# A two-layer encoder on one core: three moves in the order of the feed-forward blocks

## The chip, the core and the metric

The kernel runs on one core of one Trainium2 chip. A core has a matrix engine (PE), which multiplies and writes into PSUM banks (the kernel uses eight), a vector engine (DVE), an engine for activations and copies (ACT), a general engine (POOL), and SyncE (SP), which issues transfers. Each takes its instructions in program order and waits on semaphores of the others. The metric is the device time of one launch in microseconds (us), lower is better. Before the change the median of three runs is 2026.74 us (2025.84 to 2027.5).

## What is computed

Two layers act on 512 tokens of 1024 features. Each is a feed-forward block, a mixer, a memory attention and a second feed-forward block. The change touches only the feed-forward blocks, of which there are four:

```python
def swiglu(x, wg, wu, wd):
    return (jax.nn.silu(x @ wg) * (x @ wu)) @ wd

h = x
for layer in range(DEPTH):
    g, wg, wu, wd = ffn1[layer]
    h = h + 0.5 * swiglu(rmsnorm(h, g), wg, wu, wd)
    ...                       # mixer and memory attention
    g, wg, wu, wd = ffn2[layer]
    h = h + 0.5 * swiglu(rmsnorm(h, g), wg, wu, wd)
```

The inner width is 2816, that is 22 blocks of 128 units.

## The kernel before, in words

All activations are kept transposed, with features on the partitions and 512 tokens along a row. Every factor of a product is split into a high part and a low remainder (`wh`, `wl`, `xh`, `xl`, `t1h`, `t1l` and so on). A product is three products: high by high, low by high, high by low. The high part is an ACT copy, the low part a DVE subtraction that needs it.

A feed-forward block (`ffn`, with the prefixes l0_ffn1, l0_ffn2, l1_ffn1 and l1_ffn2 in the order of the program) walks over the 22 inner blocks in 11 pairs. Pair 0 is the plain pair: `plain_pair` multiplies it directly and leaves four PSUM banks (a gate and an up bank for each of two blocks), and `plain_end` scales the gate banks by the token factor `R` into `gs`, after which `hidden` applies silu and multiplies by the up banks. Pairs 1 to 10 save one of eight products by sums of quarters, of weights and of tokens. Each of their seven products is 24 matmuls of 128x256 (six groups of four). For a pair they are:

- `open_pair`: product "11" into bank y; ACT then copies that bank away, because y goes on collecting;
- `sum_pair`: product "1" into bank z (weights s, the sum of two quarters, made by a DMA that adds), and product "2" into y (the same s less a quarter, "second sum");
- `cross_pair`: product "21" into a bank x, product "3" into y;
- `close_pair`: product "4" into y (`lower`), product "22" into z (`upper`), then the gate of the pair.

In the trace product "1" has t1h and t1l as its first factor, "2" has t2h, "3" has t3h, "4" has t4h, and "11", "21" and "22" have xh and xl. In pair 1 the copy of y after product "11" goes straight into a quarter of the pair's result tile `gu` (L592). That tile has two buffers of one tag with `tq`, where the sums of tokens are made, so the copy also waits until `t1l` and `t2l` (L486, L488) have been made from it. In later pairs the copy goes into a PSUM bank (L595).

Between the pairs stand down products: `hh` and `hl`, the two parts of the hidden values, times the down weights `wd`, block by block into a bank (L844). The last chunk of eight inner blocks belongs to pairs 7 to 10. Its first output block has own tiles for its weights (`sh`, `sl`); in the last round `ffn` multiplies it by pairs 7 and 8, then by pair 9, the last but one, whose `hh` and `hl` have just been made (L453, L457), and then calls `close_pair` for pair 10, the final one.

What sets the order: on PE it is the order of the code. The other engines are ordered by a scheduler at build time, in which blocks under `high_priority` go ahead and `behind(ins)` keeps an instruction after another one. Three of the four blocks (all but l1_ffn1) come after an attention stage; the code calls these chained, and there the token sums of the new block are late and stand on DVE and ACT among the work of the first pair.

## Time and profile before

| What | us |
|---|---|
| median of three runs | 2026.74 (2025.84 to 2027.5) |
| the profiled execution, its own time | 2023.98 |
| span of the profiled execution, first to last instruction | 2022.0 |
| PE busy in it | 2004.7 |
| DVE busy | 1598.9 |
| ACT busy | 1278.4 |
| POOL busy | 350.0 |
| PE waiting for another engine, all groups listed | 12.0 |

The profiled execution's time is its span and 1.98 us around it, and it is 2.76 us under the median of the runs. PE is busy for 99% of the span and carries the chain of work that ended last almost alone. So a time is changed by what PE waits for, or by how fast its clock lets it go, and the profile is read there: the list of PE's waits first, then a timeline of the places where they fall.

A line of the timeline gives the start in us from the span's start, the duration, the engine, the line of code, the operation with its output and inputs, the shape and the count, and in brackets how long the engine had been idle before it and who released it. Some rows hold several instructions in a row.

### The profile page before, as it was taken

The numbers are of one execution on the slowest core, as the hardware profiler recorded it, in microseconds if no ns is written. First come the engines' busy times: TensorE is split into PE (matmuls) and PEld (weight loads), VectorE is DVE, ScalarE is ACT, GpSimd is POOL, SyncE is SP. The second block draws the span as 40 slices with busy tenths as digits, with TensorE's granted clock in tenths as the row PEclk, the third lists the DMA queues.
The fourth block names the chain that finished last, engine by engine and source line by source line (L and its number), as shares of the span: only waits on it lengthen the run. The fifth ranks groups of instructions, "written<-read, shape, count | busy, mean of one in ns | idle before, by whom it ended". The sixth has DMA issues, their size and how long they took to land.

```text
span 2022.0 us, 35264 instructions
## 1 busy us (share of the span) xinstructions
PE 2004.7 (99%) x13853; PEld 1840.3 (91%) x13853; DVE 1598.9 (79%) x2370; ACT 1278.4 (63%) x1955; POOL 350.0 (17%) x332
## 2 busy tenths in 40 slices
PE   9999999999999999999999999999999999999999
PEld 7999998888888889999989999988888888999997
DVE  8979776699676798888689798774668688979884
ACT  7766564557785566665557665645768566667572
POOL 1011001355521111000010101003453011010100
PEclk9999999999999999999999999999999999999999
DMA  7787755222331187776557877644224325777762
GB/s 234 195 218 191 197 166 160 91 89 84 103 122 64 62 237 186 207 199 170 155 176 208 209 195 198 178 139 138 84 79 136 94 74 153 205 205 197 193 183 91
DMA packets 102262, 316.52 MB, mean 157 GB/s; under 512 B 11472, under 2 KB 14672, under 8 KB 102096
## 3 DMA queue, kind: packets, MB, share of 16 engines
q1 hardware_dynamic: 85680, 257.12, 39.2%
q0 software_dynamic: 16128, 56.63, 16.2%
q8 instruction: 109, 1.79, 0.4%
q10 hardware_dynamic: 288, 0.52, 0.1%
q14 instruction: 57, 0.47, 0.1%
HBM read 301.64 MB, written 12.58 MB: 155 GB/s over the span
## 4 chain that ended last, share of the span: by engine, by line
PE 94%; DVE 3%; ACT 1%; issue 1%; DMA 0%; POOL 0%; SPq 0%; ACTq 0%; DVEq 0%; POOLq 0%
PE ps_pa L569 35%; PE ps_pb L569 14%; PE ps_pa L967 13%; PE ps_pa L913 5%; PE ps_pb L844 4%; PE ps_pa L844 4%; PE ps_pa L401 3%; PE ps_pb L1080 3%; PE ps_pa L1570 2%; PE ps_pa L1401 2%; PE ps_pb L913 2%; PE ps_pb L1133 2%; PE ps_pb L1106 1%; PE ps_pa L1300 1%; PE ps_pb L401 1%; DVE wl L546 1%
## 5 line engine op out<-in xcount | busy, mean ns | idle before, releaser
L169 ACT ACTIVATE wh<-wf 128x1024 fp32r<-128x1024 f32 (+1 forms) x155 | 154.5, 1003 | 175.8 <-issue 37.8
L544 ACT ACTIVATE wh<-s 128x1024 fp32r<-128x1024 f32 (+1 forms) x132 | 136.4, 1035 | 135.3 <-DVE s L611 43.9
L546 DVE TENSOR_TENSOR wl<-s,wh 128x1024 fp32r<-128x1024 f32 (+1 forms) x132 | 157.1, 1190 | 37.0 <-ACT wh L544 36.0
L544 ACT ACTIVATE wh<-wf 128x1024 fp32r<-128x1024 f32 (+1 forms) x132 | 134.7, 1020 | 75.5 <-PE ps_pa L569 48.0
L546 DVE TENSOR_TENSOR wl<-wf,wh 128x1024 fp32r<-128x1024 f32 (+1 forms) x132 | 154.4, 1172 | 27.2 <-ACT wh L544 27.2
L171 DVE TENSOR_TENSOR wl<-wf,wh 128x1024 fp32r<-128x1024 f32 (+1 forms) x110 | 128.7, 1175 | 41.9 <-ACT wh L169 40.1
L544 ACT ACTIVATE sh<-s 128x1024 fp32r<-128x1024 f32 (+1 forms) x92 | 94.1, 1023 | 66.9 <-PE ps_pa L569 24.6
L171 POOL TENSOR_TENSOR wl<-wf,wh 128x1024 fp32r<-128x1024 f32 (+1 forms) x45 | 99.9, 2221 | 204.9 <-ACT wh L169 142.9
L638 POOL DMA_DIRECT2D s<-l_ffn_wq x40 | 35.2, 879 | 542.9 <-ACT s L637 363.0
L546 DVE TENSOR_TENSOR sl<-s,sh 128x1024 fp32r<-128x1024 f32 (+1 forms) x92 | 108.1, 1176 | 22.7 <-ACT sh L544 22.4
L967 PE MATMUL ps_pa<-wh,xh 128*128 128x512 f32 x384 | 121.7, 398 | 0.0
L967 PE MATMUL ps_pa<-wh,xl 128*128 128x512 f32 x384 | 118.9, 391 | 0.0
L967 PE MATMUL ps_pa<-wl,xh 128*128 128x512 f32 x384 | 118.7, 390 | 0.0
L569 PE MATMUL ps_pa<-xh,wh 128*128 128x256 f32 x560 | 86.9, 276 | 0.0
L569 PE MATMUL ps_pa<-xl,wh 128*128 128x256 f32 x560 | 86.9, 276 | 0.0
L569 PE MATMUL ps_pa<-xh,wl 128*128 128x256 f32 x560 | 86.9, 276 | 0.0
L967 PEld LDWEIGHTS ps_pa<-wh,xl 128*128 128x128 f32 x384 | 72.1, 188 | 15.7
L967 PEld LDWEIGHTS ps_pa<-wl,xh 128*128 128x128 f32 x384 | 72.0, 188 | 15.5
L1095 ACT ACTIVATE e<-e,m 128x128 f32<-128x128 f32 (+3 forms) x128 | 70.7, 554 | 21.7 <-DVE m L1094 21.3
L967 PEld LDWEIGHTS ps_pa<-wh,xh 128*128 128x128 f32 x384 | 69.2, 188 | 12.3
L569 PEld LDWEIGHTS ps_pa<-xl,wh 128*128 128x128 f32 x560 | 74.2, 188 | 0.0
L569 PEld LDWEIGHTS ps_pa<-xh,wl 128*128 128x128 f32 x560 | 74.2, 188 | 0.0
(454 smaller groups left out, 6054.1 us busy)
## 6 DMA issues: line engine op xcount, KB each, us to landing
wf<-l_ffn_wq SPq DMA_DIRECT2D x120, 512.0 KB, 4.2
s<-l_ffn_wq SPq DMA_DIRECT2D x80, 512.0 KB, 4.6
s<-l_ffn_wq POOLq DMA_DIRECT2D x80, 512.0 KB, 7.4
wf<-l_w_in SPq DMA_DIRECT2D x48, 512.0 KB, 3.4
wf<-l_ffn_wd SPq DMA_DIRECT2D x32, 512.0 KB, 3.7
wf<-l_ffn_wdq SPq DMA_DIRECT2D x24, 512.0 KB, 4.3
wf<-l_ffn_wdq SPq DMA_DIRECT2D x24, 384.0 KB, 3.6
s<-l_ffn_wdq SPq DMA_DIRECT2D x16, 512.0 KB, 4.5
```

The lines of the kernel that those rows point to most:

```text
L169: self.leading = nc.scalar.activation(wh[:, sl], w[:, sl], AF.Copy)
L171: eng.tensor_sub(wl[:, sl], w[:, sl], wh.bitcast(F32)[:, sl])
L401: nc.tensor.matmul(p, w[a][:, k * P:(k + 1) * P], xs[k][c], start=k == order[0] and a == c == 0, stop=k == order[-1] and a == 1)
L544: self.leading = nc.scalar.activation(h, t, AF.Copy)
L546: self.parted = nc.vector.tensor_sub(l, t, h.bitcast(F32))
L569: self.nc.tensor.matmul(bank[:, z * 256:z * 256 + 256], w[a][:, o:o + P], xs[k][b], start=first and n == 0, stop=n == len(ops) - 1, skip_g ...
L844: self.nc.tensor.matmul(bank, w[a][:, j * P:(j + 1) * P], h, start=j == a == e == 0 and c < len(CHUNKS) - 1, stop=j == nb - 1 and (a, e) = ...
L913: nc.tensor.matmul(banks[dd], w[g, k // 2][a][:, o:o + P], parts(k)[b], start=k == first and a == b == 0, stop=k == last and a == 1)
L967: nc.tensor.matmul(banks[j], xs[k][a][:, j * P:(j + 1) * P], w[b][:, kk * 512:kk * 512 + 512], start=k == a == b == 0, stop=k == KB - 1 an ...
L1080: nc.tensor.matmul(bank[:, o:o + n], a, b[:, :n], start=c == 0, stop=c == len(ops) - 1)
L1095: nc.scalar.activation(e, e, AF.Exp, bias=m[:, i:i + 1], scale=-1.0, accum_out=rs[:, i:i + 1])
L1133: nc.tensor.matmul(p[:, q0:q0 + n], vp[jb][:, h * P:(h + 1) * P], t[:, src:src + n], start=c == 0, stop=c == 7)
```

## The change

Three edits in the feed-forward blocks.

First, the copy of pair 1's y bank goes to a tile `sq` (the tag of the squares, two buffers) in place of the corner of `gu`, under high priority; the later addition of product "21" reads it there. For the other pairs the copy keeps its place in PSUM and gets the same priority.

Second, the plain pair's gate (`gs` from banks and `R`, then silu and the products) is no longer queued by `plain_end`, which only makes `R` and leaves a function `f.gate`. `ffn` calls it after `sum_pair`, behind `f.lowered`, the low part of pair 1's second sum. `f.low(...)` of pair 2 is called a few lines later.

Third, in the last round, `close_pair` of the final pair stands ahead of the down products of pair 9.

```diff
@@ ffn
-                    self.down_products(c, early, LEAD + REST, False, range(CHUNKS[c] - 4, CHUNKS[c] - 2))
                     self.close_pair(pair, True)
+                    self.down_products(c, early, LEAD + REST, False, range(CHUNKS[c] - 4, CHUNKS[c] - 2))
                     self.down(c, early)
@@ plain_end
-        for b in range(2):
-            f.gated = nc.vector.tensor_mul(gs[:, b * S:(b + 1) * S], banks[b][0], f.R)
-        self.hidden(0, gs, [pp[1] for pp in banks])
+        def gate(after):
+            with self.behind(after):
+                for b in range(2):
+                    f.gated = nc.vector.tensor_mul(gs[:, b * S:(b + 1) * S], banks[b][0], f.R)
+            self.hidden(0, gs, [pp[1] for pp in banks])
+        f.gate = gate
@@ open_pair
-        if p == 1:
-            nc.scalar.copy(self.corner(pair, 0, 0), self.halves(pair.y))
-        else:
-            pair.x = self.bank("pa")
-            nc.scalar.copy(pair.x, pair.y)
+        with self.tc.high_priority():
+            if p == 1:
+                pair.x = self.xp.tile([P, S], F32, name="sq", tag="sq", bufs=2)
+                nc.scalar.copy(pair.x, pair.y)
+            else:
+                pair.x = self.bank("pa")
+                nc.scalar.copy(pair.x, pair.y)
@@ sum_pair
-            if p == 2:
-                f.low(f.lowered)
             f.lowered = self.parted
+            if p == 2:
+                f.low(f.lowered)
@@ cross_pair
-            nc.vector.tensor_add(c, c, self.halves(x))
+            nc.vector.tensor_add(c, self.halves(pair.x), self.halves(x))
```

The first place is DVE in pair 1 of l0_ffn1, from the low part of the token sum "2" on. `s1` holds the sums of pair 1 (its second `wl` is the low part of the second sum), `wf` a quarter as loaded, `s3` the sum for product "3", and `gs` the plain pair's gate. Before:

```order
L486 TENSOR_TENSOR t2l_440<-tq_318,t2h_438 128x1024
L424 TENSOR_TENSOR gs_383<-ps_pa_193,R_377 128x512
L424 TENSOR_TENSOR gs_383<-ps_pa_255,R_377 128x512
L486 TENSOR_TENSOR t3l_513<-tq_319,t3h_511 128x1024
L546 TENSOR_TENSOR wl_443<-s1_402,wh_442 128x1024
L546 TENSOR_TENSOR sl_474<-wf_471,sh_473 128x1024
L546 TENSOR_TENSOR wl_508<-s3_503,wh_507 128x1024
L486 TENSOR_TENSOR t4l_583<-tq_319,t4h_581 128x1024
L434 TENSOR_TENSOR gs_383<-t_386,ps_pa_194 128x512
L434 TENSOR_TENSOR gs_383<-t_386,ps_pb_256 128x512
L661 TENSOR_TENSOR s1_402<-wf_471,s1_402 128x1024
L546 TENSOR_TENSOR wl_545<-wf_542,wh_544 128x1024
```

The same twelve instructions after the change:

```order
L491 TENSOR_TENSOR t2l_424<-tq_318,t2h_422 128x1024
L551 TENSOR_TENSOR wl_427<-s1_386,wh_426 128x1024
L551 TENSOR_TENSOR sl_475<-wf_472,sh_474 128x1024
L427 TENSOR_TENSOR gs_384<-ps_pa_193,R_378 128x512
L427 TENSOR_TENSOR gs_384<-ps_pa_255,R_378 128x512
L491 TENSOR_TENSOR t3l_514<-tq_319,t3h_512 128x1024
L551 TENSOR_TENSOR wl_509<-s3_504,wh_508 128x1024
L491 TENSOR_TENSOR t4l_584<-tq_319,t4h_582 128x1024
L668 TENSOR_TENSOR s1_386<-wf_472,s1_386 128x1024
L551 TENSOR_TENSOR wl_546<-wf_543,wh_545 128x1024
L439 TENSOR_TENSOR gs_384<-t_457,ps_pa_194 128x512
L439 TENSOR_TENSOR gs_384<-t_457,ps_pb_256 128x512
```

The low part of the second sum and that of the quarter for "21" have moved ahead of the gate's first two products and of t3l, and the gate's last two products have moved behind the low part for the next pair's "11".

The second place is ACT over the same stretch, where `ps_pa_340` is bank y of pair 1 and `t` the silu of the plain pair. Before:

```order
L483 ACTIVATE t4h_581<-tq_319 128x1024
L544 ACTIVATE sh_473<-wf_471 128x1024
L544 ACTIVATE wh_442<-s1_402 128x1024
L544 ACTIVATE wh_507<-s3_503 128x1024
L592 COPY gu_374<-ps_pa_340 128x2x256
L432 ACT_TABLE_LOAD
L432 ACTIVATE t_386<-gs_383 128x1024
L544 ACTIVATE wh_544<-wf_542 128x1024
L619 COPY gu_374<-ps_pa_340 128x2x256
```

And after:

```order
L488 ACTIVATE t4h_582<-tq_319 128x1024
L549 ACTIVATE sh_474<-wf_472 128x1024
L599 COPY sq_375<-ps_pa_340 128x512
L549 ACTIVATE wh_426<-s1_386 128x1024
L549 ACTIVATE wh_508<-s3_504 128x1024
L549 ACTIVATE wh_545<-wf_543 128x1024
L626 COPY gu_374<-ps_pa_340 128x2x256
L437 ACT_TABLE_LOAD
L437 ACTIVATE t_457<-gs_384 128x1024
```

The copy of y has moved ahead of the high parts of the second and third sums, and the table load with the silu behind the next pair's first high part and the second copy of y.

The third place is PE in the last round. `ps_pa<-hh,sh` are down products, `ps_pb<-xh,wh` begins product "22" of the final pair, and `t4h` is in its product "4". Before:

```order
L844 MATMUL ps_pa<-hh,sl 128x512 x4
L844 MATMUL ps_pa<-hh,sh 128x512 x2
L844 MATMUL ps_pa<-hl,sh 128x512 x2
L844 MATMUL ps_pa<-hh,sl 128x512 x2
L569 MATMUL ps_pb<-xh,wh 128x256 x4
```

And after, at the end of that pair:

```order
L574 MATMUL ps_pa<-t4l,wh 128x256 x4
L574 MATMUL ps_pa<-t4h,wl 128x256 x4
L851 MATMUL ps_pa<-hh,sh 128x512 x2
L851 MATMUL ps_pa<-hl,sh 128x512 x2
L851 MATMUL ps_pa<-hh,sl 128x512 x2
```

The six down products of pair 9 have moved behind the 48 matmuls that close the final pair. This is the only move on PE; it is made in all four blocks.

## The prediction

> **What bounds the kernel now.** I read the page first: busy time, then the chain that ended last.

> ```profile
> PE 2004.7 (99%) x13853; PEld 1840.3 (91%) x13853; DVE 1598.9 (79%) x2370; ACT 1278.4 (63%) x1955; POOL 350.0 (17%) x332
> PE 94%; DVE 3%; ACT 1%; issue 1%; DMA 0%; POOL 0%; SPq 0%; ACTq 0%; DVEq 0%; POOLq 0%
> ```

> PE is the bound, and the change removes no matmul. What it can win is time in which PE waits, so the next view is the list of waits, PE alone (total us, times, longest):

> ```profile
> PE ps_pa L569 <- ACT gu L592: 5.0, 3, 1.7
> PE ps_pa L569 <- DVE wl L546: 2.7, 3, 0.9
> PE ps_pa L844 <- DVE hl L457: 1.8, 4, 0.5
> PE ps_pa L569 <- ACT gu L644: 0.5, 1, 0.5
> ```

> These make 10.0 us, and all of them lie where the change works. The first two fall together, once in each chained block; the timeline of l0_ffn1 shows how:

> ```profile
> 32.94 1.04 ACT L544 ACTIVATE sh<-wf 128x1024 fp32r<-128x1024 f32 x1
> 35.49 1.22 DVE L486 TENSOR_TENSOR t2l<-tq,t2h 128x1024 fp32r<-128x1024 f32 x1
> 35.60 2.01 ACT L544 ACTIVATE wh<-s 128x1024 fp32r<-128x1024 f32 x2 [1.63 <-DVE s L611]
> 36.63 1.28 DVE L424 TENSOR_TENSOR gs<-ps_pa,R 128x512 f32<-128x512 f32 x2
> 37.52 0.56 ACT L592 COPY gu<-ps_pa 128x512 f32<-128x512 f32 x1
> 38.13 0.73 PE L569 MATMUL ps_pa<-t2h,wh 128*128 128x256 f32 x4 [1.66 <-ACT gu L592]
> 38.96 1.22 DVE L546 TENSOR_TENSOR wl<-s,wh 128x1024 fp32r<-128x1024 f32 x1
> 40.23 0.72 PE L569 MATMUL ps_pa<-t2h,wl 128*128 128x256 f32 x4 [0.91 <-DVE wl L546]
> ```

> PE had finished product "1" at 38.13 - 1.66 = 36.47. Product "2" adds to bank y, so it waited for ACT to copy y away, and that copy stood behind two high parts. Then it waited for the low part of its weights, which on DVE stood behind the gate's first two products and t3l.

> A stall has a second price in the third chained block, l1_ffn2. The chain has the same 112 matmuls after the stall in l0_ffn1 and in l1_ffn2 (start, us):

> ```profile
> 40.23 12.96 PE ps_pa L569 x112
> 1720.15 14.62 PE ps_pa L569 x112
> ```

> The windows say why (PE busy, then the other engines, then PEclk, the granted clock):

> ```profile
> 41.00:42.00 1.00, 1.00 (x11) 1.00 (x10) 1.00 (x2) 0.10 (x1) 0.00 (x0) 1.00 0.00 0
> 1721.00:1722.00 1.00, 1.00 (x7) 1.00 (x7) 1.00 (x2) 0.00 (x0) 0.00 (x0) 0.50 0.00 0
> ```

> After the stall of l1_ffn2 the clock was granted at 0.50; this cost 14.62 - 12.96 = 1.66 us. It happened after one of three like stalls. [...]

> **The change part by part.** First the copy of y. Behind `sh<-wf` (ends 32.94 + 1.04 = 33.98) ACT was idle for 1.63 us before 35.60, and PE had ended product "11" by then. The copy to `sq` needs about the 0.56 us of its old row and fits whole into that gap: it costs nothing. Were the gap gone, it would cost 0.56 us. Product "2" then needs only its high part, the first of the two at 35.60, ready at about 35.60 + 1.05 = 36.65. With the 0.05 us that a hand-over takes (copy ends 38.08, PE starts 38.13), PE starts at 36.70 and not at 38.13.

> Second, the gate. DVE now takes the low part of the second sum where the gate's products stood, at 36.65, and has it at 36.65 + 1.22 = 37.87, so PE can use it from 37.92. PE gets there at 36.70 + (40.23 - 0.91 - 38.13) = 37.89. Product "2" thus goes on at 37.92 and not at 40.23, which is 2.3 us earlier, with 0.2 us of waiting left in front of the high part.

> What is late next? DVE, which works without a break through the whole pair. The rows that follow:

> ```profile
> 43.50 0.68 DVE L434 TENSOR_TENSOR gs<-t,ps_pa 128x512 f32<-128x512 f32 x1
> 46.97 0.42 DVE L706 TENSOR_TENSOR t<-gs 128x256 f32<-128x256 f32 x1
> 47.30 0.68 DVE L630 TENSOR_TENSOR gu<-gu,ps_pa 128x512 f32<-128x512 f32 x1
> 47.90 1.22 DVE L546 TENSOR_TENSOR sl<-wf,sh 128x1024 fp32r<-128x1024 f32 x1
> 50.31 0.62 PE L569 MATMUL ps_pa<-t4h,sh 128*128 128x256 f32 x4
> 51.22 0.62 PE L569 MATMUL ps_pa<-t4h,sl 128*128 128x256 f32 x4
> ```

> The low part `sl` for product "4" keeps its place on DVE: the same work stands ahead of it, less L706, which moves behind (a slot of 47.30 - 46.97 = 0.33 us). It ends at 47.90 - 0.33 + 1.22 = 48.79. PE needs it at 51.22 - 2.3 = 48.9. The slack of 2.1 us falls to 0.1 us. Pair 2's own second sum is as thin, since DVE now has one more low part to make ahead of it. Between a gain of nothing and the whole slack used up I put 0.15 us per block for these two, with ends of 0 and 1.1 us (one more DVE step of 1.14, 36.63 - 35.49, in the way). So a chained block wins 2.3 - 0.15 = 2.15 us.

> The gate itself gets later: its last products move from 43.50 to about 45.8, behind two more DVE steps of 1.14. Who waits for them is the copy of pair 2's y into a bank that the first of them frees, at the head of ACT's queue. It comes after pair 2's product "11", about 50.31 - 2.3 = 48.0, so 1.5 us of cover is left.

> In l0_ffn2 the product "4" also waited for a copy, because ACT had the plain pair's hidden parts ahead of it:

> ```profile
> 745.18 0.64 ACT L716 ACTIVATE th<-t 128x512 fp32r<-128x512 f32 x1
> 746.67 0.56 ACT L644 COPY gu<-ps_pa 128x512 f32<-128x512 f32 x1
> 747.29 0.74 PE L569 MATMUL ps_pa<-t4h,sh 128*128 128x256 f32 x4 [0.47 <-ACT gu L644]
> ```

> These come later with the gate, so 0.47 us goes too. In l1_ffn1 there is nothing to win: DVE made the low part at 1056.80, ahead of the gate already, and PE did not wait:

> ```profile
> 1056.80 1.23 DVE L546 TENSOR_TENSOR wl<-s,wh 128x1024 fp32r<-128x1024 f32 x1
> 1061.36 0.62 PE L569 MATMUL ps_pa<-t2h,wh 128*128 128x256 f32 x4
> ```

> Third, the closing of the final pair, here in l0_ffn1; the other three look alike:

> ```profile
> 288.47 0.68 DVE L645 TENSOR_TENSOR gu<-gu,ps_pb 128x512 f32<-128x512 f32 x1
> 289.07 1.22 DVE L457 TENSOR_TENSOR hl<-gs,hh 128x1024 fp32r<-128x1024 f32 x1
> 289.27 0.63 PE L844 MATMUL ps_pa<-hh,sh 128*128 128x512 f32 x2
> 290.35 0.73 PE L844 MATMUL ps_pa<-hl,sh 128*128 128x512 f32 x2 [0.45 <-DVE hl L457]
> ```

> PE multiplied with `hh` at 289.27 and stood 0.45 us for `hl`. Now product "22" begins at 289.27. The last that it needs is the read of bank z, done at 288.47 + 0.68 = 289.15, so the cover is 0.07 us after the hand-over. The six down products follow 48 matmuls (5.4 us) later, long after `hl` is there (290.29). The final pair's gate comes 1.8 us earlier, ahead of down products that stay last. This wins 4 x 0.45 = 1.8 us, with ends of 1.2 and 1.8.

> Transfers: the third sum of pair 2 is fetched, negated by ACT, added to by a DMA from POOL, and read by ACT.

> ```profile
> 42.47 0.33 SPq L554 DMA_DIRECT2D s<-l_ffn_wq  x1
> 48.82 1.06 ACT L637 ACTIVATE s<-s 128x1024 f32<-128x1024 f32 x1
> 50.18 0.92 POOL L638 DMA_DIRECT2D s<-l_ffn_wq  x1 [17.74 <-DVE t L706]
> 58.27 1.07 ACT L544 ACTIVATE wh<-s 128x1024 fp32r<-128x1024 f32 x1 [1.34 <-PE ps_pb L569]
> s<-l_ffn_wq SPq DMA_DIRECT2D x80, 512.0 KB, 4.6
> s<-l_ffn_wq POOLq DMA_DIRECT2D x80, 512.0 KB, 7.4
> ```

> The fetch is there at 42.47 + 4.6 = 47.1, so the negation can start 1.7 us earlier than 48.82, and the sum lands at 50.18 - 1.7 + 7.4 = 55.9; ACT wants it at 58.27 - 2.3 = 56.0. That just holds, and PE uses it three products later.

> The sum: 3 x 2.15 + 0.47 + 1.8 = 8.7 us, plus the halved clock. I take the one in three of the profiled execution, 1.66 us. On the profiled execution that gives 2023.98 - 8.7 - 1.66 = 2013.6. The median of the runs stands 2.76 us above it; I leave that as it is: **2016.4 us**. [...]

> **The rivals.** (a) The clock was halved after all three stalls in the timed runs; the 2.76 us between them and the profiled execution speak for it, the single slow stretch in the trace against. Then 3 x 1.66 = 5.0 go: 2026.74 - 8.7 - 5.0 = 2013.0.

> (b) DVE becomes the bound of the first pair: with the slack of 0.1 us above, one more DVE step in the way per block takes half of the 2.15. For it: DVE has no gap from 35.49 to 47.90. Against: its work there shrinks by the one L706. 2026.74 - (3 x 1.1 + 0.47 + 1.8) - 1.66 = 2019.5.

> (c) The 2.15 us are paid back at the next transfers: the third sum has 0.1 us of cover, and if the DMA sets the pace, PE only waits elsewhere. Against: PE's list of waits has no DMA in it. Left are 1.8 us and the clock, 2026.74 - 1.8 - 1.66 = 2023.3, no difference that counts (0.2%, 4.1 us, is about what a measurement of this kernel can tell from no change).

> (d) Slower: the gate comes too late for ACT. If its last products start after 47.3, the copy of pair 2's y stops ACT's queue, and behind it stand the high parts for pair 2's products. From there each us is a us of PE. To lose 2 us net per chained block it must be 2.15 + 2 late, at 51.5 and not 45.8, and the clock halves after each: 2026.74 + 3 x 2 - 1.8 + 2 x 1.66 = 2034.3. Nothing in the rows makes the silu 5.7 us late.

> That the moves are not made can be ruled out, as the order shows them.

> **Numbers.** Forecast 0.60, (a) 0.12, (b) 0.14, (c) 0.10, (d) 0.04. All but (c) and (d) are faster by over 0.2%: 0.86; same 0.10; slower 0.04. The range runs from just under (a), 2012.8, to beyond (b), 2020.8.

> **What would show it.** In the new profile PE's waits should hold neither the copy of y nor `hl`, and for `wl` or `sl` under 1 us in all, against 10.0 us for the four lines above; DVE's low part of the second sum should start about 36.7 in l0_ffn1; the granted clock should be 1.00 in all three first pairs. Wrong would be a new wait of PE of 1 us or more in pairs 1 or 2, a wait for a transfer, or a span that shrinks by less than the waits that went.

## The result and the profile after

| What | us |
|---|---|
| changed kernel, median of four runs | 2016.02 (2014.49 to 2017.71) |
| kernel before, median of four runs | 2027.12 (2025.84 to 2029.69) |
| ratio, with its 95% interval | 0.9944 [0.9927, 0.9961] |
| forecast (range) | 2016.4 (2012.8 to 2020.8) |

The change is 11 us faster, 0.6%. The profiled execution took 2017.71 us and was the longest of the four, while that of before (2023.98) was shorter than all four of its runs: between the two profiles lie only 6.3 us. So the profile has to say first what came and went by chance, and then what the change did. (Beside the experiments below the kernel before ran 61 more times; one of these took 5225.3 us and is left out of the means.)

The busy time of the page has not moved (PE 2004.7 before); it is the waits that did. Below stand the busy line of the changed kernel and its list of PE's waits (total us, times, longest). Two lines that both kernels have are left out: 1.6 us at the very start and 0.2 us near 1550.

```profile
PE 2004.5 (99%) x13853; PEld 1840.5 (91%) x13853; DVE 1596.4 (79%) x2370; ACT 1277.8 (63%) x1955; POOL 349.6 (17%) x332
PE ps_pa L574 <- ACT wh L549: 2.1, 5, 0.8
PE ps_pa L401 <- ACT xh L233: 1.4, 3, 0.8
PE ps_pb L574 <- ACT sh L549: 0.7, 1, 0.7
```

The four lines of the prediction (the copy of y, `wl`, `hl`, the copy at product "4"), 10.0 us together, are all gone. Three stand in their place. The first is in part what was foreseen: 0.24, 0.33 and 0.27 us in front of product "2" of the chained blocks. The rest of it, and `sh`, fall in pair 4 of l0_ffn1 and l1_ffn1, where nothing waited before. The line of `xh` is at the start; before, it was 0.2 us.

The first pair of l0_ffn1, by the timeline:

```profile
35.33 0.69 DVE L421 COPY R<-ps_pb 128x512 f32<-128x512 f32 x1
35.47 0.57 ACT L599 COPY sq<-ps_pa 128x512 f32<-128x512 f32 x1
35.94 1.22 DVE L618 TENSOR_TENSOR s<-s,wf 128x1024 f32<-128x1024 f32 x1
37.19 2.01 ACT L549 ACTIVATE wh<-s 128x1024 fp32r<-128x1024 f32 x2 [1.16 <-DVE s L618]
38.28 1.23 DVE L551 TENSOR_TENSOR wl<-s,wh 128x1024 fp32r<-128x1024 f32 x1
38.30 0.74 PE L574 MATMUL ps_pa<-t2h,wh 128*128 128x256 f32 x4 [0.24 <-ACT wh L549]
39.56 0.74 PE L574 MATMUL ps_pa<-t2h,wl 128*128 128x256 f32 x4
49.23 1.21 DVE L551 TENSOR_TENSOR sl<-wf,sh 128x1024 fp32r<-128x1024 f32 x1
50.58 0.65 PE L574 MATMUL ps_pa<-t4h,sl 128*128 128x256 f32 x4
```

Between product "2" with `wh` and with `wl` lie 1.26 us, where there were 2.10. The copy of y sits in ACT's gap, ahead of the high parts. The low part `sl` of product "4" ends at 49.23 + 1.21 = 50.44 and PE uses it at 50.58: 0.14 us of slack is left. This execution was 1.58 us late when it came to the pair; less that, the low part of the second sum starts at 38.28 - 1.58 = 36.70, where the prediction had it at about 36.7. (l0_ffn1 is the first stage of the program: the code counts it among the chained blocks, but no attention stage stands before it, and its x arrives in pieces from memory.)

The clock was granted in full behind all three of these places (the window of l1_ffn2 that answers to the one of before at 0.50):

```profile
1717.00:1718.00 1.00, 1.00 (x11) 1.00 (x10) 1.00 (x3) 0.54 (x1) 0.00 (x0) 1.00 0.15 61
```

At the closing of l0_ffn1 I compare starts, from the last down product ahead of it to the first of the next output block. Before:

```profile
288.35 1.08 PE L844 MATMUL ps_pa<-hh,sl 128*128 128x512 f32 x4
...
290.91 0.62 PE L844 MATMUL ps_pa<-hh,sl 128*128 128x512 f32 x2
...
296.88 1.32 PE L844 MATMUL ps_pb<-hh,wh 128*128 128x512 f32 x5
```

And after:

```profile
289.00 1.08 PE L851 MATMUL ps_pa<-hh,sl 128*128 128x512 f32 x4
...
295.44 0.62 PE L851 MATMUL ps_pa<-hh,sh 128*128 128x512 f32 x2
295.90 0.62 PE L851 MATMUL ps_pa<-hl,sh 128*128 128x512 f32 x2
...
296.81 1.52 PE L851 MATMUL ps_pb<-hh,wh 128*128 128x512 f32 x6
```

The same matmuls take 8.53 us before and 7.81 after, 0.72 less, though the row of the wait was 0.45.

Taking such differences of starts along the whole of both profiles, the account is this. Won: 2.10 in the first pair of l0_ffn1, 2.95 and 0.16 in l0_ffn2, 3.89 in l1_ffn2 (1.66 of it the clock), and 0.71 + 0.65 + 0.67 + 0.74 = 2.77 at the four closings, 11.87 in all. Lost: 1.57 at the start, 1.17 in pair 4 of l0_ffn1, 2.43 in l1_ffn1, 0.49 in l1_ffn2, 5.66 in all. The difference, 6.21, is that of the two spans.

The loss at the start lies where both kernels issue the same instructions in the same order. The windows show it: x came late in this execution (the line of `xh`) and the clock was halved, where it had been full before. The columns are the stretch, its length, then PE, PEld, DVE, ACT and POOL busy, PEclk, the DMA share and GB/s. After, then before:

```profile
9.00:10.00 1.00, 1.00 (x3) 0.81 (x4) 1.00 (x2) 1.00 (x3) 0.00 (x0) 0.50 1.04 391
```

```profile
9.00:10.00 1.00, 1.00 (x6) 0.73 (x5) 1.00 (x3) 1.00 (x3) 0.00 (x0) 1.00 1.03 385
```

Over the 13 profiles of this study product "1" of l0_ffn1 starts at 33.1 to 33.9 us in six and at 35.1 to 35.6 in seven. The seven are those with a halved clock there. Six of the eight profiles of kernels with both the copy and the gate moved are among them, all three of the unaltered changed kernel too, and one of the five others. The timed runs say that it is not in every execution of the changed kernel: six of its 14 runs show a mean granted clock of 1.000 (a halved stretch of 3.41 us alone would take 0.0008 off), and they took 2014.67 us in the mean, against 2016.35 for the eight at 0.999. That it is chance and has nothing to do with the change is not shown.

### The profile page after: what moved, and what is told of

Same layout as the page of the kernel before. It is cut to its first block, busy times and chain, and to the rows that moved or that the text cites. A ratio compares the mean times of both kernels' runs of the same rounds, so it can differ in the third digit from the quotient of the medians.

```text
span 2015.8 us, 35265 instructions
## 1 busy us (share of the span) xinstructions
PE 2004.5 (99%) x13853; PEld 1840.5 (91%) x13853; DVE 1596.4 (79%) x2370; ACT 1277.8 (63%) x1955; POOL 349.6 (17%) x332
## 4 chain that ended last, share of the span: by engine, by line
PE 95%; DVE 2%; ACT 1%; issue 1%; DMA 1%; POOL 0%; SPq 0%; ACTq 0%; POOLq 0%; DVEq 0%
PE ps_pa L574 35%; PE ps_pb L574 13%; PE ps_pa L974 13%; PE ps_pa L920 5%; PE ps_pa L851 4%; PE ps_pb L851 4%; PE ps_pa L401 3%; PE ps_pb L1087 3%; PE ps_pa L1577 2%; PE ps_pa L1408 2%; PE ps_pb L920 2%; PE ps_pb L1140 2%; PE ps_pb L1113 1%; PE ps_pa L1307 1%; PE ps_pb L401 1%
## 5 line engine op out<-in xcount | busy, mean ns | idle before, releaser
L645 POOL DMA_DIRECT2D s<-l_ffn_wq x40 | 35.2, 880 | 538.9 <-ACT s L644 350.1
L574 PEld LDWEIGHTS ps_pa<-xh,wh 128*128 128x128 f32 x560 | 74.2, 188 | 0.0
## 6 DMA issues: line engine op xcount, KB each, us to landing
wf<-l_ffn_wq SPq DMA_DIRECT2D x120, 512.0 KB, 4.5
s<-l_ffn_wq SPq DMA_DIRECT2D x80, 512.0 KB, 4.6
s<-l_ffn_wq POOLq DMA_DIRECT2D x80, 512.0 KB, 7.7
wf<-l_w_in SPq DMA_DIRECT2D x48, 512.0 KB, 3.4
wf<-l_ffn_wd SPq DMA_DIRECT2D x32, 512.0 KB, 3.7
wf<-l_ffn_wdq SPq DMA_DIRECT2D x24, 512.0 KB, 4.5
s<-l_ffn_wdq SPq DMA_DIRECT2D x16, 512.0 KB, 4.3
```

What stands on the lines that cost most here:

```text
L574: self.nc.tensor.matmul(bank[:, z * 256:z * 256 + 256], w[a][:, o:o + P], xs[k][b], start=first and n == 0, stop=n == len(ops) - 1, skip_g ...
```

## The experiments

Theory: the copy and the gate hold the same product one behind the other, so either alone wins little; each closing gives back its wait; and DVE is left with 0.1 us to spare. The rivals stand with each run. Times are medians; ratios are against runs of the kernel before on the same chip, and a gain in us that stands behind a ratio is worked out from it.

**Copy alone.** The kernel before with the copy to `sq` and its priority, and no other edit.

```diff
-            nc.scalar.copy(self.corner(pair, 0, 0), self.halves(pair.y))
+                pair.x = self.xp.tile([P, S], F32, name="sq", tag="sq", bufs=2)
+                nc.scalar.copy(pair.x, pair.y)
```

> Only the copy of pair 1's y bank is moved (to a tile of squares, under high priority); gate and closing stand as before. My theory, the two moves need each other: product '2' of a chained block starts 1.4 us earlier, but DVE still makes the low part of its weights behind the gate's two products and t3l, so product '2' stands there and goes on at the same time as before. PE's list: the wait for the copy (5.0 us) is gone, the wait for wl grows from 2.7 to about 3 x 2.3 = 6.9 us. Time against before: no gain, 0 +- 0.7 us, ratio 1.000. Rival, the waits add up: 3 x 1.66 = 5.0 us go, ratio 0.9975. On the clock: one pause of 2.3 us stands in place of two; if such pauses can halve it, some of the three places show 0.50 behind them, at 1.66 us each.

Measured: 2027.59 us, ratio 1.0006 [0.9997, 1.0015]: no gain. Its list of PE's waits:

```profile
PE ps_pa L569 <- DVE wl L546: 6.9, 3, 2.3
PE ps_pa L569 <- ACT wh L544: 0.8, 3, 0.3
```

The 5.0 us of the copy have become 4.2 more for `wl` and 0.8 for `wh`, 5.0 again, as the theory said. And behind two of the three pauses of 2.31 us the clock was halved:

```profile
43.00:44.00 1.00, 1.00 (x7) 1.00 (x6) 1.00 (x2) 0.73 (x2) 0.00 (x0) 0.50 0.52 74
739.00:740.00 1.00, 1.00 (x7) 1.00 (x6) 1.00 (x2) 0.00 (x0) 0.00 (x0) 0.50 0.00 0
1724.00:1725.00 1.00, 1.00 (x12) 1.00 (x11) 1.00 (x1) 0.39 (x1) 0.00 (x0) 1.00 0.00 0
```

**Gate alone.** The gate behind `f.lowered`, with `f.low` of pair 2 after it; copy and closing as before.

```diff
-        for b in range(2):
-            f.gated = nc.vector.tensor_mul(gs[:, b * S:(b + 1) * S], banks[b][0], f.R)
-        self.hidden(0, gs, [pp[1] for pp in banks])
+        f.gate = gate
```

> Only the plain pair's gate is moved behind the low part of the second sum; copy and closing stand as before. My theory: product '2' still starts when ACT has copied bank y behind two high parts, so the 3 x 1.66 us stay; the low part is there by then, so the 0.9 us go in each chained block, and the 0.47 us of the copy in l0_ffn2. Time against before: 3.2 us less, ratio 0.9984. Rival, the low part's place is what holds the pair and the copy only a symptom: 2.1 us or more per chained block, 6.5 us, ratio 0.9968.

Measured: 2023.03 us, ratio 0.9985 [0.9976, 0.9994], 3.0 us of 2025.71. Its waits:

```profile
PE ps_pa L574 <- ACT gu L597: 5.0, 3, 1.7
PE ps_pa L574 <- ACT wh L549: 1.4, 2, 0.8
PE ps_pa L574 <- DVE wl L551: 0.4, 2, 0.2
```

The copy still takes its 1.7 us three times; the wait for `wl` at product "2" is gone (the 0.4 us that are listed fall at a later product with `xh`, in l0_ffn2 and l1_ffn2), and so is that of the copy at product "4" in l0_ffn2. That is the theory's number. So copy 0 and gate 3.0 alone, and 6.7 together (below): the copy needs the gate. The line of `wh` is new, in pair 4 of l0_ffn1 and l1_ffn1, and is followed up below.

**Closing alone.**

```diff
+                    self.close_pair(pair, True)
                     self.down_products(c, early, LEAD + REST, False, range(CHUNKS[c] - 4, CHUNKS[c] - 2))
-                    self.close_pair(pair, True)
```

> Only the six down products of pair 9 are moved behind the products that close the final pair, in all four blocks. Theory of the prediction: the four rows of the list go, 4 x 0.45 = 1.8 us, ratio 0.9991. Rival, from the stage's length in the two profiles: between the product ahead and the first down product behind, the stage takes 8.53 us before and 7.81 after, so a pause costs about 0.25 us beside its row (matmuls at its edges take longer): 4 x 0.7 = 2.8 us, ratio 0.9986. The stage's length in this run's profile tells them apart: 8.08 or 7.8 us. The first pairs' pauses of 1.66 and 0.91 us stay.

Measured: 2022.29 us, ratio 0.9988 [0.9979, 0.9998], 2.4 us. The time cannot tell 1.8 from 2.8; the starts can. Measured against the profile of before, the four closings are 0.71, 0.62, 0.63 and 0.68 us shorter, 2.64 in all: the rival was right, each of these pauses cost more than its row of 0.45. The wait for `hl` has left the list. Behind the two later first-pair stalls, which stay here, the clock was halved:

```profile
738.00:739.00 1.00, 1.00 (x5) 1.00 (x6) 1.00 (x2) 0.10 (x1) 0.00 (x0) 0.50 0.00 0
1725.00:1726.00 1.00, 1.00 (x6) 1.00 (x6) 1.00 (x3) 0.88 (x2) 0.00 (x0) 0.50 0.23 57
```

**Copy and gate.** The changed kernel with the two lines of the closing put back in their old order.

> The whole change but for the closing, which is put back as before. My theory: copy and gate together win 2.1 to 2.3 us in each of three chained blocks and 0.5 us more in l0_ffn2, beside 1.66 us for every place where the clock was halved: 7.0 us without the clock, about 8.6 with it, ratio 0.9957, and the four waits for hl (1.8 us) are in the list again. Rival, the three moves gain together only (the closing needs the earlier gate or the other way round): the sum of this run's gain and that of the closing alone differs from the gain of the whole, 11 us, by more than 2 us.

Measured: 2019.29 us, ratio 0.9967 [0.9955, 0.9979], 6.7 us, near the 7.0 expected without the clock (8.6 with it, 0.9957, lie inside the interval too); the four waits for `hl` (1.8 us) are back. With the closing's 2.4 this makes 9.1 against 11 for the whole: within the 2 us that were set, and the intervals are wider than that.

**The changed kernel again.** Unaltered, with a second profile.

> The changed kernel once more, unaltered, for a second profile and more times. Its first profiled execution was the longest of four and lost 1.57 us in its first 13 us (x late, then a clock of 0.50) and some 2 us in waits for transfers in pair 4 of l0_ffn1 and l1_ffn1. Theory, the change leaves pair 4 with less cover for its transfers in every run: the waits for ACT's wh and sh in pair 4 are there again, 0.5 us or more in l0_ffn1 and l1_ffn1. Rival, they are chance of one execution, like the late start: gone here. Time: 2015 to 2017 us, ratio 0.9955 by the sum of copy and gate (0.9967) and closing (0.9988); PE waits 0.25 to 0.35 us in front of product '2' in each chained block; the granted clock is 1.00 behind these short pauses.

Measured: 2015.12 us, ratio 0.9944 [0.9930, 0.9957]. Waits of 0.4 us in pair 4 of l0_ffn1, a little short of the 0.5 expected, and 0.8 in l1_ffn1 are there again; so is the late start. The clock was 1.00 behind all three first pairs.

**R copied by ACT.** The changed kernel, with one instruction moved from DVE to ACT.

```diff
-            nc.vector.tensor_copy(f.R, p)
+            nc.scalar.copy(f.R, p)
```

> The changed kernel with the copy of the token factor R out of its bank made by ACT, in the gap behind the copy of y, and not by DVE ahead of the second sum. My theory: what is left in front of product '2' (0.24 to 0.33 us for the high part, about 0.2 us more for the low part, three times) hangs on DVE's chain, which R's copy of 0.6 us heads; without it the second sum is there 0.6 us earlier, these waits go and 'sl' for product '4' gains 0.6 us of cover. Gain against the changed kernel 3 x 0.45 = 1.4 us, ratio to before 0.995 where the changed kernel has 0.9955: hardly to be told by times, but PE's list has no wait of 0.2 us or more for wh at product '2'. Rival, ACT's queue is the tight one there: the high parts come 0.5 us later behind the extra copy and the wait grows to 0.8 us.

Measured: 2016.24 us, ratio 0.9950 [0.9938, 0.9963], no better than the changed kernel. In l0_ffn1 the wait in front of product "2" is gone, but in l0_ffn2 and l1_ffn2 it grew to 0.56 and 0.44 us. The timeline of l0_ffn2 says why:

```profile
728.43 1.22 DVE L618 TENSOR_TENSOR s<-s,wf 128x1024 f32<-128x1024 f32 x1
728.94 1.04 ACT L488 ACTIVATE t4h<-tq 128x1024 fp32r<-128x1024 f32 x1
729.88 0.56 ACT L599 COPY sq<-ps_pa 128x512 f32<-128x512 f32 x1
730.35 0.58 ACT L421 COPY R<-ps_pb 128x512 f32<-128x512 f32 x1
730.83 2.01 ACT L549 ACTIVATE wh<-s 128x1024 fp32r<-128x1024 f32 x2
731.94 0.74 PE L574 MATMUL ps_pa<-t2h,wh 128*128 128x256 f32 x4 [0.56 <-ACT wh L549]
```

The second sum was ready at 729.65, and now ACT, with t4h ahead of the two copies, was the late one. The rival held in two of three blocks.

**One more DVE step, after and before.** The low part of the token sum "4" is made twice, into the same tile; this edit was put into the changed kernel and into the kernel before.

```diff
-                    nc.vector.tensor_sub(l, t, h.bitcast(F32))
+                    for _ in range(2 if name == "t4" else 1):
+                        nc.vector.tensor_sub(l, t, h.bitcast(F32))
```

> The changed kernel with the low part of the token sum '4' made twice (one more DVE step of 1.14 us in each first pair, ahead of product '4'). By the prediction DVE has 0.1 us of slack left at product '4': PE then stands 1.0 to 1.5 us for t4l or sl in each chained block, 3 to 4.5 us in all, ratio to before some 0.997 to 0.998 where the changed kernel has 0.9955. Rival, DVE still has the room it had before the change (2.1 us): no wait, no change of time.

> The kernel before with the same extra DVE step ahead of product '4'. Its slack there was 2.1 us: the step fits, PE's list has no new wait of 0.2 us or more at product '4' and the time stays within 0.5 us, ratio 1.000. If the step costs here as much as in the changed kernel, the slack was not what the change used up. The pauses of 1.66 and 0.91 us stay, so this profile gives three more samples of the clock behind them: 0.50 in about half.

Measured in the changed kernel: 2019.04 us, ratio 0.9966 [0.9952, 0.9979], some 4 us lost. Its list has

```profile
PE ps_pa L575 <- DVE t4l L492: 4.1, 3, 1.4
```

and in l0_ffn1 the rows are

```profile
47.47 1.22 DVE L552 TENSOR_TENSOR sl<-wf,sh 128x1024 fp32r<-128x1024 f32 x1
48.60 1.22 DVE L492 TENSOR_TENSOR t4l<-tq,t4h 128x1024 fp32r<-128x1024 f32 x1
49.88 0.72 PE L575 MATMUL ps_pa<-t4l,sh 128*128 128x256 f32 x4 [1.35 <-DVE t4l L492]
```

The second `t4l` stands behind `sl` here, and PE wants it one row (0.45 us) ahead of `sl`. So the wait is longer than the 1.14 us of the step less the slack.

In the kernel before, where the second `t4l` stands ahead of `sl`: ratio 1.0000 [0.9989, 1.0010], and no line for t4l. Its waits in pair 1 are those of before, to the tenth; a single one of 0.4 us for `sl` in pair 2 of l1_ffn2 is new. So before the change the step fitted into slack, and in the changed kernel it does not: with it DVE sets the pace at product "4" of each chained block. All three of its clocks were 1.00 behind the stalls of 1.66 and 0.91 us.

**The hidden parts' call as before.** The changed kernel, with one line of its diff undone.

```diff
+            if p == 2:
+                f.low(f.lowered)
             xs = self.tokens("2")
             w = self.operand(pair.s)
             f.lowered = self.parted
-            if p == 2:
-                f.low(f.lowered)
```

> The changed kernel with the call for the plain pair's hidden parts in pair 2 back where it was, ahead of the low part of the second sum. Seen so far: PE waits 0.5 to 0.8 us for ACT's wh at product '2' of pair 4 in l0_ffn1 (about 126 us) and in l1_ffn1 (about 1146 us) in all profiles of kernels that have the gate moved by the change alone (gate_alone, copy_and_gate, the changed kernel twice), and 0.2 us or less in the four that keep the gate. Theory: the waits come of the hidden parts of pairs 1 to 3, which the later call pushes back on ACT and DVE; with it back, both waits fall to 0.2 us or less, and about 1.5 us are won against the changed kernel (ratio to before 0.9937 where that one has 0.9944). Rival: they come of PE being earlier against transfers that keep their pace; then both waits stay at 0.5 us or more. First pairs as in the changed kernel, 0.25 to 0.35 us in front of product '2'.

Measured: 2017.58 us, ratio 0.9964 [0.9951, 0.9976], 3 us more than the changed kernel on the same chip (2014.60). Pair 4's waits for `wh` are gone, but pair 2 of each chained block now waits for its own low part:

```profile
PE ps_pa L574 <- DVE sl L551: 2.7, 3, 0.9
PE ps_pa L574 <- ACT wh L549: 0.8, 3, 0.3
```

So this line of the change, which the prediction did not price by itself, is worth 2.7 us of waits: without it the slack of pair 2's second sum is not thin but missing.

**The changed kernel a third time**, beside that one.

> The changed kernel a third time, beside the kernel above on one chip: 2015 to 2016 us, the waits of pair 4 there again in l0_ffn1 and l1_ffn1 with 0.5 us or more each, 0.25 to 0.35 us in front of product '2' of each chained block, the clock at 1.00 behind them. By chance alone (the rival of the second profile) at least one of the two waits of pair 4 would be gone.

Measured: 2014.60 us, ratio 0.9948 [0.9934, 0.9962]. The wait in l1_ffn1 was there (0.7 us), the one in l0_ffn1 was not. By the sign set beforehand this speaks for chance in l0_ffn1: the wait is not in every execution of one and the same kernel.

**The early call in l1_ffn1 alone.**

```diff
+            early = p == 2 and f.pre == "l1_ffn1_"
+            if early:
+                f.low(f.lowered)
```

> The changed kernel with the old, early call for the plain pair's hidden parts in l1_ffn1 alone, the block without a pause in its first pair; the three chained blocks keep the call of the change. Theory from the two runs before: the early call takes away pair 4's wait in l1_ffn1 (0.5 to 0.8 us in PE's list, 1 to 2.4 us in the starts around it) and costs 0.9 us for sl in pair 2 only where the block is chained. So no wait for sl in pair 2, none of 0.3 us or more in l1_ffn1, and 1 to 1.5 us won against the changed kernel: ratio to before about 0.994, where that one had 0.9944 to 0.9948. Rival, pair 4's wait in l1_ffn1 comes of the transfers' pace and was absent by chance: it is there again with 0.5 us or more, and the time is that of the changed kernel.

Measured: 2015.79 us, ratio 0.9940 [0.9927, 0.9954], the changed kernel's time. The wait in l1_ffn1 is there as large as ever. The first row is the issue of two fetches, of which the first is that of the third sum:

```profile
1133.54 2.42 SPq L559 DMA_DIRECT2D s<-l_ffn_wq  x2
1139.67 1.06 ACT L647 ACTIVATE s<-s 128x1024 f32<-128x1024 f32 x1 [2.55 <-DMA s<-l_ffn_wq]
1145.87 0.74 PE L574 MATMUL ps_pa<-t2h,wh 128*128 128x256 f32 x4 [0.80 <-ACT wh L549]
```

My theory of the hidden parts falls: in this kernel DVE and ACT run the whole of l1_ffn1 in the order of the kernel before, but for the copy to `sq`, and the wait still came. What the rows show is the near cause: the negation of a third sum (its fetch lands late; ACT stands 2.55 us for it) is at the head of ACT's queue, and behind it stand the high parts that PE needs. In the kernel before, where PE did not wait, the same place is

```profile
1135.84 2.42 SPq L554 DMA_DIRECT2D s<-l_ffn_wq  x2
1140.68 1.06 ACT L637 ACTIVATE s<-s 128x1024 f32<-128x1024 f32 x1 [1.26 <-DMA s<-l_ffn_wq]
1144.32 0.62 PE L569 MATMUL ps_pb<-t1h,sh 128*128 128x256 f32 x4
```

The fetch is issued 1144.32 - 1135.84 = 8.48 us ahead of PE's product "1", and in the kernel with the early call, where that product starts at 1142.02, just as far: 1142.02 - 1133.54 = 8.48. But the negation starts 4.84 us behind the issue before and 6.13 us here. So PE does not come earlier against this fetch; the fetch itself takes longer to land.

## Why the prediction was right, point by point

**The copy and the gate in the chained blocks.** Foreseen: 2.15 us for each and 0.47 more in l0_ffn2. Measured: 2.10 in l0_ffn1, 2.95 + 0.16 in l0_ffn2 (0.5 more than foreseen), 3.89 - 1.66 = 2.23 in l1_ffn2; nothing in l1_ffn1's first pair. The remaining 0.2 us in front of the high part was measured at 0.24 to 0.33. Copy alone and gate alone show that the step "then it waited for the low part" was read rightly: two waits in a row, the second of which, 2.31 us by itself, showed only 0.9 us behind the first.

**What is late next.** Foreseen: `sl` for product "4" with 0.1 us of slack out of 2.1. Measured: 0.14. The extra DVE step bears both out: a step of 1.14 us fitted into the slack before, and in the changed kernel it made PE wait 1.4 us in each chained block. That pair 2's own second sum "is as thin" was right too, but it holds only because the call for the hidden parts was moved.

**The closing.** The mechanism was right; the term was too small, 1.8 us where the starts give 2.64 to 2.77. The row of a wait is idle time alone. In the kernel before, from the first of the six down products (289.27) to the second (290.35) it is 1.08 us, of which 0.45 are the row; the other 0.63 stand against 295.90 - 295.44 = 0.46 in the full stream of the changed kernel. Behind the pause 290.91 - 290.35 = 0.56 stand against 0.46 again. Both edges together are the missing 0.27.

**The clock.** Foreseen: one halving of 1.66 us goes. The two stalls of 1.66 and 0.91 us stand unchanged in the profiles of the kernel before, of closing alone and of the kernel before with the DVE step: the clock was halved after three of nine, one per execution in the mean (1, 2 and 0). That the one profile at hand had just this mean is luck. Rival (a), all three in one execution, was seen in no profile.

The timed runs have no trace, but each lists its mean granted clock. Of the 60 of the kernel before beside the experiments 30 show 0.999 or 1.000, 24 show 0.998 and 6 less; the 14 of the changed kernel show 0.999 or 1.000. The means lie 0.0010 apart, some 2.0 us of the span, where 1.66 were foreseen (an estimate, from clocks that are rounded to 0.001, and with the start and the end of an execution in them). Three halved stretches, as in rival (a), would bring the mean clock to 0.9975, and 54 of the 60 runs show 0.998 or more.

**Transfers.** Foreseen: "That just holds", at pair 2, and it does: no wait there. Not foreseen: pair 4. Nine of the profiles are of kernels with the moved gate, four of kernels with the old one. A wait of 0.4 us or more for ACT's `wh` in pair 4 stands in l0_ffn1 in six of the nine, in l1_ffn1 in eight of the nine, and in neither block in any of the four. This is the part of rival (c) that came true. It took back, in the first profile, 1.17 and 2.43 us. So errors of the sum stand against each other: the closing undervalued by about 0.9 us and l0_ffn2 by 0.5, and pair 4 at nothing where it costs more than both in the first profile. That the forecast came within 0.4 us of the median is in part luck. Two of the prediction's own signs of being wrong did appear: a wait that goes back to a transfer, and a span that shrank by 6.2 us where 10.0 us of waits went (1.57 of the difference is the late start).

Why the third sum is late in pair 4 stays open. The order inside the block is excluded as the cause in l1_ffn1, and by the rows above so is a PE that comes earlier while the fetch is issued no sooner. What goes with the wait in every profile is the time of the fetch from issue to landing. In l1_ffn1 it is 4.59 to 5.27 us in the five profiles without the wait and 5.33 to 6.69 in the eight with it; in l0_ffn1 3.88 to 5.03 in seven and 5.14 to 5.71 in six. What makes the fetch slower no run here shows.

**The 2.76 us** between profile and median of before were left as they were, and that was right: the profile of before had no late start, which costs some 2 us in seven of thirteen profiles. The timed runs show one part of it by their clocks: the 26 runs of the kernel before at 0.999, the clock of its profile, took 2025.05 us in the mean, and the 24 at 0.998 took 2026.94. At equal clock the changed kernel is 8.7 us shorter at 0.999 (eight runs) and 9.3 at 1.000 (six against four), where the prediction had 8.7 for the waits alone; these runs are few and from several chips.

Rival (b), one DVE step in the way, was the nearest: it is what the kernel becomes if a single instruction is added. Rival (d) had nothing for it: in l0_ffn1 of the changed kernel the bank that the gate frees first was read by 48.12, and the copy of pair 2's y came at 50.39 with ACT busy up to it. No variant was shown to be faster than the changed kernel.

## What to carry to other kernels

When two waits stand one behind the other on the same product, price them together: removing the first alone won nothing here, removing the second alone only its own row. Behind a wait that goes, look for the slack of the next low part in the queue, here 0.1 us of 2.1, and say that it is now the limit. The row of a wait can be less than what it costs: here rows of 0.45 us stood for 0.62 to 0.74 us at the closings, where the edges of the pause came on top, and a halved clock behind a pause took 1.66 us more.

## What was not expected of the hardware

The granted clock fell to 0.50 behind pauses that were much shorter than the time for which it fell (3.41 us, once 6.82): after two of three pauses of 2.31 us (with 0.25 ahead of them), after three of nine pairs of 1.66 and 0.91 us, and after none of three single pauses of 1.66 to 1.69 us or three of 1.36 us.

```profile
1717.09:1720.51 3.42, 1.56 (x11) 1.37 (x12) 3.42 (x5) 3.25 (x4) 0.00 (x0) 1.00 0.61 198
1720.51:1723.92 3.41, 3.41 (x19) 3.41 (x18) 3.41 (x4) 1.09 (x2) 0.00 (x0) 0.50 0.18 14
734.05:737.47 3.42, 2.12 (x15) 1.92 (x16) 3.42 (x4) 2.68 (x3) 0.00 (x0) 1.00 0.43 159
737.47:740.88 3.41, 3.41 (x33) 3.41 (x32) 3.41 (x5) 1.53 (x2) 0.00 (x0) 1.00 0.28 53
```

In l1_ffn2 PE was busy for 1.56 of 3.42 us and the next stretch ran at half; in l0_ffn2 it was busy for 2.12 and the next ran in full.

At the start, where x arrives in pieces and PE waits 0.2 to 1.3 us up to several times, the clock fell in seven of thirteen profiles, and product "1" then came some 2 us later. There the idle time does not sort the cases: the stretch ahead held 1.08 to 1.59 us of it in the seven (1.36 in the first profile of the changed kernel), and 1.33 in one profile that kept its clock.
